# Projections and gates of three chunks in scaled fp16 parts, with the weights' parts kept in DRAM

## The chip, the cores and the metric

The kernel runs on one core of a Trainium2 chip. The metric is the time of one execution on the device in microseconds (us), the median of several runs. Engines are named as in the profile: PE (TensorE), PEld (its weight loads), DVE (VectorE), ACT (ScalarE), POOL (GpSimd) and SP (SyncE), which issues the DMAs.

## The reference, cut to what matters

One layer of a decoder trunk over 2048 tokens and 1024 channels, in float32. A normalised input h goes through one projection whose columns serve three token mixers and three merge gates; the three branches are merged by the gates, and a feed-forward part follows.

```python
h = rmsnorm(x, norm_mix_g[l])
proj = h @ w_in[l]
(lru_x, lru_gate, m_qk, m_v, m_o, m_i, m_f,
 s_q, s_k, s_v, g_a, g_b, g_c) = jnp.split(proj, split_points, axis=-1)
...
merged = (jax.nn.sigmoid(g_a) * ya + jax.nn.sigmoid(g_b) * yb
          + jax.nn.sigmoid(g_c) * yc)
x = x + merged @ w_o[l]

hf = rmsnorm(x, norm_ffn_g[l])
gate, up = jnp.split(hf @ w_ffn_in[l], 2, axis=-1)
x = x + (jax.nn.silu(gate) * up) @ w_ffn_out[l]
```

g_a, g_b and g_c are 1024 columns each, the other parts 2312 together.

## The kernel before, in words

The tokens are cut into four chunks of 512 (CH), the channels into eight groups of 128 (KT). Every product of the mixers works on two parts of each operand, a high and a low one, whose sum is the float32 value: `dense` (L194) issues three matmuls per group of channels, high by high, high by low, low by high, all in fp32r (the type that the program gives to 4-byte float operands of PE). A weight tile of 128 x 1024 holds one output group of 128 columns for all eight channel groups, so one output tile takes 24 matmuls of 512 columns.

`weights` (L183) makes the two parts of a weight tile: SP loads the raw tile (two buffers), ACT rounds it to the high part `wh` (L173), DVE subtracts to get the low part `wl` (L181); `wh` and `wl` have three buffers each. This happens anew for every chunk. `h_of_chunk` (L307) normalises the input of a chunk and splits it in the same way (`hh`, `hl`).

`S` (L313) makes the projections of a chunk: 14 tiles with `proj` (L336, weights wS, PSUM tile psd), and two token-major products with `tproj` (L342), in which a slice of h is the stationary operand and 264 columns (wMV) or 256 columns (wSV) of weights move; each of these has two weight tiles. So 18 weight tiles per chunk. In chunk 0 the input isn't normalised yet, and the results are scaled by the row R afterwards. The mLSTM, the LRU and the attention of the chunk before run beside it. `G` (L1042) makes the gates: for each of eight output groups one tile wY with the branches' outputs (py, six matmuls per branch), and for each of three branches one tile wG (pg, 24 matmuls), a sigmoid and the merge: 24 wG tiles per chunk. `G_out` (L1078) multiplies by wO (po) and adds the input. The feed-forward part (`F1`, `F2`) already works in fp16: `wforms` (L788) scales its weights by a power of two that is found from the sum of their squares (`squares`, `exponent`, `power`) and splits them with `split2` (L779) into two fp16 parts; `product` (L868) multiplies. Its input is prepared beside the gates of chunks 2 and 3 (`input_first`, L951: it loads fq with L944, DVE, POOL and ACT work on it).

The program is written as one sequence; a scheduler that knows each instruction's data and buffers then sets the order on every engine and on the DMA queue of SP. Pools of buffers set which tile waits for which reader. The instructions of each engine, and the DMAs that SP issues, stand in one line each.

Of the kernel before, what the change touches and what calls it, by code (L numbers as in the profile page):

```python
# [18 lines left out]
P = 128  # L19
# [15 lines left out]

class Trunk:
# [10 lines left out]
    def setup(self):  # L47
# [19 lines left out]
        self.dX1 = dr.tile([NCH, KT, P, CH], F32, name="dX1")  # L67
        self.dRow = dr.tile([NCH, 2, 4, CH], F32, name="dRow")
# [4 lines left out]
        self.rs2 = [cp.tile([P, NB], F32, name=f"rs2{c}") for c in range(NCH)]  # L73

# [104 lines left out]
    def split(self, hi, lo, src, eng, pool=False):  # L179
        self.hi(hi, src, eng)  # L180
        (self.nc.gpsimd if pool else self.nc.vector).tensor_tensor(lo, src, hi.bitcast(F32), op=ALU.subtract)  # L181

    def weights(self, src, ncol):  # L183
        wp = self.wp
        raw = wp.tile([P, WCOL], F32, tag="wraw", name="wraw", bufs=2)
        wh = wp.tile([P, WCOL], FR, tag="wh", name="wh", bufs=3)
        wl = wp.tile([P, WCOL], FR, tag="wl", name="wl", bufs=3)
        with self.first(self.HP & 1):
            self.nc.sync.dma_start(raw[:, :ncol], src)
            self.split(wh[:, :ncol], wl[:, :ncol], raw[:, :ncol], "P" if self.turn("wh", self.WH if self.phase == "S" else self.WG) else "A",  # L190
                       self.turn("wl", self.WL if self.phase == "S" else 0.0))
        return wh, wl

# [86 lines left out]
    def h_unscaled(self):  # L280
# [4 lines left out]
        for k in range(KT):  # L285
            if k % 4 == 2:
                self.w0.append(self.weights(self.I["wMV"][k // 4], 1056))
# [19 lines left out]
    def h_of_chunk(self, c):  # L307
# [3 lines left out]
        return self.make_h(p, lambda k: self.x_tile(c, k), self.g1, R, lambda k: [p.tile([P, CH], FR, tag="h" + e, name="h" + e, bufs=self.NH) for e in "hl"])  # L311

    def S(self, c, hs, at=None):  # L313
# [15 lines left out]
        def scaled(ps):  # L329
            if not at:  # L330
                return ps
            t = mp.tile([P, CH], F32, tag="cv", name="scl", bufs=1)
            V.tensor_tensor(t, ps, R, op=ALU.mult)  # L333
            return t

        def proj(i):  # L336
            w = self.weights(I["wS"][i], 1024)
# [4 lines left out]
        def tproj(name, n, per, after=None):  # L342
            pss = []
            ws = self.w0 if after else [self.weights(I[name][u], 4 * n) for u in range(2)]
# [25 lines left out]
        def mv(b, ps):  # L370
            r = rs[:, b : b + 1] if at else 1.0
# [7 lines left out]
        tproj("wMV", 264, mv, first_stat if at else None)  # L379
        st["vaug"], st["ifb"] = vaug, ifb  # L380

        def halo(tag, j, ps):
# [7 lines left out]
            else:  # L390
                A.activation(x[:, 3:], ps, AF.Copy)
# [12 lines left out]
        for j in range(4):  # L404
            x = halo("xm", j, proj(4 + j))
# [8 lines left out]
        for j in range(2):  # L414
            ps = scaled(proj(8 + j))
            o = mp.tile([P, CH], F32, tag=f"so{j}", name=f"so{j}", bufs=1)
            A.activation(o, ps, AF.Sigmoid)
            st["so"].append(o)
        def s_lru():
            st["xa"] = mp.tile([P, 2, CH], F32, tag="xa", name="xa", bufs=1)  # L420
            st["gl"] = mp.tile([P, 2, CH], F32, tag="gl", name="gl", bufs=1)
            for j in range(2):
                x = halo("xl", j, proj(10 + j))
                conv(st["xa"][:, j], x, self.cw_lru[:, j, :])
            for j in range(2):
                ps = scaled(proj(12 + j))
                t = mp.tile([P, CH], F32, tag="sg", name="gt", bufs=1)
                A.activation(t, ps, AF.Square)
# [3 lines left out]
                V.tensor_tensor(st["gl"][:, j], t, ps, op=ALU.mult)  # L432

        def s_sb():

            for i in range(4):
                ps = scaled(proj(i))
                th = mp.tile([P, CH], FR, tag="sth", name="sth", bufs=1)
                tl = mp.tile([P, CH], FR, tag="stl", name="stl", bufs=1)
                self.split(th, tl, ps, "A")  # L440
# [4 lines left out]
            def sv(b, ps):  # L445
                tv = mp.tile([P, 4, P], FR, tag="sth", name="sv", bufs=1)
                src = ps[:, :256]
                if at:
                    src = mp.tile([P, CH], F32, tag="cv", name="svs", bufs=1)[:, :256]
                    A.activation(src, ps[:, :256], AF.Copy, scale=rs[:, b : b + 1])  # L450
                src = src.rearrange("p (h d) -> p h d", h=4)
                self.split(tv[:, :, 0:64], tv[:, :, 64:128], src, "A")
                nc.sync.dma_start(self.dV[c * NB + b], tv.bitcast(F32))

            tproj("wSV", 256, sv)
# [265 lines left out]
    def F_constants(self):  # L721
# [13 lines left out]
        self.goff = row("goff", 197.0)  # L735
        self.gs2, self.offh2 = self.input_scale(self.g2, "2")
# [305 lines left out]
    def G(self, c, hs, steps=0):  # L1042
# [209 lines left out]
    def run(self):  # L1252
# [6 lines left out]
        with ExitStack() as s0:  # L1259
            with ExitStack() as s1:  # L1260
# [195 lines left out]
```

## Time and profile before

| | |
|---|---|
| median of 3 runs | 2951.1 us (2948.3 to 2951.5) |
| the profiled execution | 2951.2 us, its span 2949.5 us |
| PE busy | 2827.9 us, 96% of the span, 13409 matmuls |
| DVE busy | 1994.5 us, 68% |
| ACT busy | 1362.6 us, 46% |
| POOL busy | 782.2 us, 27% |
| read from and written to HBM | 310.9 MB and 87.6 MB |

The span goes from the first to the last instruction. The busy time of PE is modelled: matmuls follow each other in a pipeline and their records overlap, so that the pace of PE is read from the number of matmuls that start in a stretch, or from the starts themselves. In time the kernel has four parts: projections with the mixers to about 650 us (chunk 1 roughly from 150 to 310, chunk 2 to 485, chunk 3 to 650), the gates of chunks 0 and 1 beside the last attention to about 1115, the gates of chunks 1 to 3 with little beside them to about 1650, and the feed-forward part to the end.

### The profile page before, as it was taken

How to read it: one execution, taken by the hardware profiler on the slowest of the kernel's cores; microseconds unless marked ns; L12 is line 12 of the kernel's file. 1: busy time of each engine (PE TensorE's matmuls, PEld its weight loads, DVE VectorE, ACT ScalarE, POOL GpSimd, SP SyncE). 2: the span in 40 equal slices, each digit the busy share in tenths (PEclk: the TensorE clock that was granted, in tenths of full speed). 3: DMA queues.
4: the chain of work that ended last, by engine and by line, in shares of the span. 5: the costliest groups of instructions: out<-in, count | busy, mean ns of one | idle time of the engine just before them, and what ended most of it. 6: DMA issues, size and time to landing. Idle time of an engine off the chain costs nothing.

```text
span 2949.5 us, 37052 instructions
## 1 busy us (share of the span) xinstructions
PE 2827.9 (96%) x13409; PEld 1866.0 (63%) x13409; DVE 1994.5 (68%) x2933; ACT 1362.6 (46%) x2122; POOL 782.2 (27%) x916
## 2 busy tenths in 40 slices
PE   8999999998999999999999989999999999799996
PEld 7777878787887887878887534444444444344443
DVE  7678888988678775564444787556666665557557
ACT  4445554655455553333323466445554454335332
POOL 0122322332223220130001564223333333223221
PEclk9999999999999999999999999999999999999998
DMA  5445545345345325534433332122222226438324
GB/s 174 149 161 174 168 136 180 124 140 185 100 133 186 119 83 195 166 105 144 154 99 137 120 111 93 56 77 80 87 84 79 84 85 248 155 150 325 149 97 143
DMA packets 165271, 400.99 MB, mean 136 GB/s; under 512 B 19520, under 2 KB 40000, under 8 KB 156384
## 3 DMA queue, kind: packets, MB, share of 16 engines
q1 hardware_dynamic: 165088, 398.63, 39.5%
q8 instruction: 105, 1.72, 0.2%
q14 instruction: 78, 0.64, 0.1%
HBM read 310.93 MB, written 87.62 MB: 135 GB/s over the span
## 4 chain that ended last, share of the span: by engine, by line
PE 80%; DVE 8%; DMA 4%; issue 3%; ACT 2%; POOL 2%; SPq 0%; DVEq 0%; POOLq 0%; ACTq 0%
PE pfp L875 7%; PE pfp L876 7%; PE pfp L877 7%; PE pg L202 5%; PE pg L201 5%; PE pg L200 5%; PE pfq L875 3%; PE pfq L876 3%; PE pfq L877 3%; PE psd L200 3%; PE psd L202 3%; PE psd L201 3%; PE pt L707 2%; PE pfr L875 2%; PE pfr L876 2%
## 5 line engine op out<-in xcount | busy, mean ns | idle before, releaser
L181 DVE TENSOR_TENSOR wl<-wraw,wh 128x768 fp32r<-128x768 f32 (+2 forms) x232 | 287.5, 1240 | 245.7 <-ACT wh L173 237.7
L173 ACT ACTIVATE wh<-wraw 128x768 fp32r<-128x768 f32 (+2 forms) x232 | 238.9, 1030 | 433.8 <-PE pg L201 199.6
L875 PE MATMUL pfp<-f,wh 128*128 128x512 f16 x1056 | 403.3, 382 | 30.3 <-ACT wh L784 12.9
L876 PE MATMUL pfp<-f,wh 128*128 128x512 f16 x1056 | 403.2, 382 | 2.3 <-DVE f L782 2.3
L877 PE MATMUL pfp<-f,wl 128*128 128x512 f16 x1056 | 400.7, 381 | 0.0
L875 PEld LDWEIGHTS <-wh 128*128 128x128 f16 x1848 | 181.6, 98 | 248.7 <-ACT wh L784 19.1
L876 PEld LDWEIGHTS <-wh 128*128 128x128 f16 x1848 | 181.7, 98 | 235.1 <-issue 27.6
L877 PEld LDWEIGHTS <-wl 128*128 128x128 f16 x1848 | 181.4, 98 | 224.4 <-issue 9.0
L202 PE MATMUL pg<-hh,wl 128*128 128x512 f32 x768 | 307.1, 400 | 3.7 <-DVE wl L181 3.5
L200 PE MATMUL pg<-hh,wh 128*128 128x512 f32 x768 | 305.5, 398 | 3.1 <-ACT wh L173 3.1
L201 PE MATMUL pg<-hl,wh 128*128 128x512 f32 x768 | 305.7, 398 | 0.0
L802 POOL TENSOR_TENSOR sm<-raw 128x512 f32<-128x512 f32 (+1 forms) x50 | 67.5, 1350 | 592.7 <-DVE wl L785 271.7
L875 PE MATMUL pfq<-f,wh 128*128 128x512 f16 x528 | 201.5, 382 | 1.5 <-DVE xf L1188 1.0
L876 PE MATMUL pfq<-f,wh 128*128 128x512 f16 x528 | 201.4, 381 | 1.2 <-DVE f L782 1.2
L877 PE MATMUL pfq<-f,wl 128*128 128x512 f16 x528 | 200.4, 380 | 0.0
L200 PE MATMUL psd<-hh,wh 128*128 128x512 f32 x448 | 184.7, 412 | 3.2 <-DVE scl L333 2.7
L202 PE MATMUL psd<-hh,wl 128*128 128x512 f32 x448 | 180.1, 402 | 0.0
L201 PE MATMUL psd<-hl,wh 128*128 128x512 f32 x448 | 179.7, 401 | 0.0
L784 ACT ACTIVATE wh<-raw,scf 128x512 f16<-128x512 f32 (+1 forms) x166 | 127.1, 781 | 113.9 <-DVE scf L776 104.5
L202 PEld LDWEIGHTS pg<-hh,wl 128*128 128x128 f32 x768 | 145.5, 189 | 38.7 <-DVE wl L181 6.1
L200 PEld LDWEIGHTS pg<-hh,wh 128*128 128x128 f32 x768 | 146.3, 191 | 36.4 <-ACT wh L173 3.9
L201 PEld LDWEIGHTS pg<-hl,wh 128*128 128x128 f32 x768 | 145.6, 190 | 33.5
(318 smaller groups left out, 6232.9 us busy)
## 6 DMA issues: line engine op xcount, KB each, us to landing
wraw<-in_wG SPq DMA_DIRECT2D x96, 512.0 KB, 3.5
dA<-fs SPq DMA_DIRECT2D x154, 256.0 KB, 2.0
f<-dA SPq DMA_DIRECT2D x22, 1792.0 KB, 10.9
wraw<-in_wS SPq DMA_DIRECT2D x56, 512.0 KB, 3.8
raw<-in_wF SPq DMA_DIRECT2D x26, 1024.0 KB, 4.7
x<-in_xT SPq DMA_DIRECT2D x88, 256.0 KB, 3.8
wraw<-in_wO SPq DMA_DIRECT2D x32, 512.0 KB, 5.2
raw<-in_wP SPq DMA_DIRECT2D x16, 1024.0 KB, 6.7
```

Source lines behind the costliest of these rows:

```text
L173: nc.scalar.activation(dst, src, AF.Copy)
L181: (self.nc.gpsimd if pool else self.nc.vector).tensor_tensor(lo, src, hi.bitcast(F32), op=ALU.subtract)
L200: nc.tensor.matmul(ps, wh, hh, start=start and i == 0, stop=False)
L201: nc.tensor.matmul(ps, wh, hl, start=False, stop=False)
L202: nc.tensor.matmul(ps, wl, hh, start=False, stop=stop and i == n - 1)
L707: PE.transpose(pt[:, i * P : (i + 1) * P], As[i][:, js], self.idn)
L784: self.nc.scalar.activation(hi, x, AF.Copy, scale=s)
L802: G.tensor_tensor(sm[:, 0], a21, a22, op=ALU.add)
L875: mm(ps, wh[:, i, ks], f[:, j, 0], start=start and k == 0, stop=False, skip_group_check=True)
L876: mm(ps, wh[:, i, ks], f[:, j, 1], start=False, stop=False, skip_group_check=True)
L877: mm(ps, wl[:, i, ks], f[:, j, 0], start=False, stop=k == n - 1, skip_group_check=True)
```

## The change

Chunk 0 works as before, but ACT also squares each of its 42 raw tiles that chunks 1 to 3 use again (2 wMV, 2 wSV, 14 wS, 24 wG), into one column of `kacc` each. From these columns `weight_scales` finds a power of two per tile, in four calls: one small matmul with a tile of ones that sums over the partitions, and five to seven small DVE operations. `ksc` is the scale of a tile, `kinv` what its product is multiplied by.

In chunks 1 to 3 h is made in fp16 parts, with a scaled gain (`gs1`). Chunk 1 loads each raw tile, scales and splits it into two fp16 parts, both in one tile `w16`, and writes that tile to `dW` in DRAM. Chunks 2 and 3 load it from there, with one DMA of the same size as the raw tile; their buffers alternate between the two tags, six in all. What reads the products out of PSUM applies `kinv` as a scale: in ACT's activations and in DVE operations that take a factor. The products py and po, with wY and wO, stay as they were. The diff, cut to its core:

```diff
+        self.dW = dr.tile([NKEY, P, 2, WCOL], F16, name="dW")
...
-    def weights(self, src, ncol):
-        wp = self.wp
+    def weights(self, src, ncol, key=None, c=0):
+        nc, wp = self.nc, self.wp
+        if key is not None and c:
+            w = wp.tile([P, 2, WCOL], F16, tag="wl" if c > 1 and self.turn("w", 0.5) else "wh", name="w16", bufs=3)
+            wh, wl = w[:, 0, :ncol], w[:, 1, :ncol]
+            if c == 1:
+                raw = wp.tile([P, WCOL], F32, tag="wraw", name="wraw", bufs=2)
+                nc.sync.dma_start(raw[:, :ncol], src)
+                self.split2(wh, wl, raw[:, :ncol], self.ksc.bitcast(F32)[:, key : key + 1])
+                nc.sync.dma_start(self.dW[key, :, :, :ncol], w[:, :, :ncol])
+            else:
+                nc.sync.dma_start(w[:, :, :ncol], self.dW[key, :, :, :ncol])
+            return wh, wl
...
+        if key is not None:
+            self.squares(raw[:, :ncol], self.kacc[:, key : key + 1], raw[:, :ncol])
         return wh, wl
+
+    def weight_scales(self, k0, k1, pair=None):
+        nc, V = self.nc, self.nc.vector
+        n = k1 - k0
+        ps = self.psum("m", "pse")
+        nc.tensor.matmul(ps[:, :n], self.ones16, self.kacc[:, k0:k1], start=True, stop=True)
...
-        return self.make_h(p, lambda k: self.x_tile(c, k), self.g1, R, lambda k: [p.tile([P, CH], FR, tag="h" + e, name="h" + e, bufs=self.NH) for e in "hl"])
+        g, dt = (self.gs1, F16) if c else (self.g1, FR)
+        return self.make_h(p, lambda k: self.x_tile(c, k), g, R, lambda k: [p.tile([P, CH], dt, tag="h" + e, name="h" + e, bufs=self.NH) for e in "hl"])
...
-            w = self.weights(I["wS"][i], 1024)
+            w = self.weights(I["wS"][i], 1024, KS + i, c)
...
-                A.activation(x[:, 3:], ps, AF.Copy)
+                A.activation(x[:, 3:], ps, AF.Copy, scale=self.inverse(KS + i))
...
-                V.tensor_tensor(t, t, ps, op=ALU.mult)
+                V.scalar_tensor_tensor(t, ps, r, t, op0=ALU.mult, op1=ALU.mult)
...
-                w = self.weights(I["wG"][br * KT + j], 1024)
+                w = self.weights(I["wG"][br * KT + j], 1024, KG + br * KT + j, c)
...
-                    A.activation(sg, pg, AF.Sigmoid)
+                    A.activation(sg, pg, AF.Sigmoid, scale=self.inverse(KG + br * KT + j) if c else 1.0)
...
+                                    if c == 0:
+                                        self.weight_scales(KMV, KMV + 2, KMV)
+                                        self.weight_scales(KS + 4, KS + 14)
                                     st["sb"]()
+                                    if c == 0:
+                                        self.weight_scales(KSV, KS + 4, KSV)
...
+                    if c == 0:
+                        self.weight_scales(KG, NKEY)
                     self.G_out(c, mer, 3 if c == NCH - 1 else 0)
```

The scheduler orders the changed program anew. Two places on SP's queue show it. In the projections of chunk 1, toward the rows of the mLSTM (dRow), raw weight tiles (wraw) were loaded in a run, before:

```order
L189 DMA wraw<-in_wS 128x1024
L277 DMA x<-in_xT 128x512 x2
L189 DMA wraw<-in_wS 128x1024 x6
L558 DMA dRow<-sg 4x512
L559 DMA dRow<-yh 4x512
```

and now:

```order
L206 DMA dW<-w_2213 256x1x1024
L204 DMA wraw<-in_wS 128x1024
L206 DMA dW<-w_2253 256x1x1024
L204 DMA wraw<-in_wS 128x1024
L614 DMA dRow<-sg 4x512
L615 DMA dRow<-yh 4x512
```

Each load of a raw tile has got a write of fp16 parts (w with a number is the tile w16) just ahead of it.

At the start of the gates of chunk 2, where the input of the feed-forward part (fq) is loaded between the weights, before:

```order
L189 DMA wraw<-in_wY 128x768
L944 DMA fq<-dX_81 128x512
L189 DMA wraw<-in_wG 128x1024
L944 DMA fq<-dX_81 128x512 x2
L189 DMA wraw<-in_wG 128x1024
L944 DMA fq<-dX_81 128x512 x3
L189 DMA wraw<-in_wG 128x1024
```

and now:

```order
L208 DMA w_12534<-dW 128x2x1024
L1001 DMA fq<-dX_81 128x512 x2
L213 DMA wraw<-in_wY 128x768
L1001 DMA fq<-dX_81 128x512 x2
L208 DMA w_12586<-dW 128x2x1024
L1001 DMA fq<-dX_81 128x512 x2
L208 DMA w_12623<-dW 128x2x1024
```

The loads of wG have become reads of dW into the tiles that PE takes; they still share the queue with the loads of fq.

## Rows read from the trace of the kernel before

**Rows 1.** The page: busy us, share and instructions of each engine; the chain.
```profile
PE 2827.9 (96%) x13409; PEld 1866.0 (63%) x13409; DVE 1994.5 (68%) x2933; ACT 1362.6 (46%) x2122; POOL 782.2 (27%) x916
...
PE 80%; DVE 8%; DMA 4%; issue 3%; ACT 2%; POOL 2%; SPq 0%; DVEq 0%; POOLq 0%; ACTq 0%
```
**Rows 2.** By stage: us; PE, PEld, DVE, ACT, POOL busy (count); clock, DMA share, GB/s.
```profile
150.00:310.00 160.00, 151.35 (x806) 124.73 (x806) 124.24 (x201) 80.11 (x138) 45.09 (x75) 0.95 0.50 160
310.00:485.00 175.00, 167.47 (x901) 139.33 (x899) 146.22 (x226) 96.01 (x167) 51.93 (x91) 0.94 0.50 165
485.00:650.00 165.00, 159.49 (x858) 130.57 (x859) 144.02 (x216) 93.65 (x163) 47.81 (x90) 0.97 0.45 139
1450.00:1600.00 150.00, 150.00 (x646) 121.30 (x645) 59.41 (x72) 43.58 (x58) 0.00 (x0) 1.00 0.30 93
1800.00:2400.00 600.00, 599.88 (x2810) 272.07 (x2809) 371.86 (x558) 304.84 (x438) 191.34 (x136) 1.00 0.22 81
```
**Rows 3.** By stage, the scale sums (tile pse) on PE alone.
```profile
1800.00:2400.00 600.00, 5.68 (x34) 1.00 0.22 81
```
**Rows 4.** Groups of matmuls by line and form: busy us, mean ns, idle before.
```profile
L202 PE MATMUL pg<-hh,wl 128*128 128x512 f32 x768 | 307.1, 400 | 3.7 <-DVE wl L181 3.5
...
L200 PE MATMUL psd<-hh,wh 128*128 128x512 f32 x448 | 184.7, 412 | 3.2 <-DVE scl L333 2.7 <-DVE stl L181 0.5
...
L352 PE MATMUL psd<-wh,hh 128*128 128x264 f32 x128 | 40.6, 327 | 11.5 <-ACT wh L173 8.7 <-DVE ifb L373 2.4 <-ACT hh L173 0.4
```
**Rows 5.** PE in order of time, chunk 2's wMV: first and last of 18.
```profile
316.36 0.28 PE L353 MATMUL psd<-wl,hh 128*128 128x264 f32 x1
...
318.42 0.28 PE L352 MATMUL psd<-wh,hh 128*128 128x264 f32 x1
```
**Rows 6.** Groups: the two halves of a split, an accumulator's read, a scale sum.
```profile
L173 ACT ACTIVATE wh<-wraw 128x1024 fp32r<-128x1024 f32 x192 | 203.1, 1058 | 342.2 <-PE pg L201 175.1 <-PE psd L201 85.2 <-PE po L201 48.3
...
L181 DVE TENSOR_TENSOR wl<-wraw,wh 128x1024 fp32r<-128x1024 f32 x192 | 244.7, 1275 | 187.2 <-ACT wh L173 179.3 <-ACT yt L716 6.1 <-DMA dY<-ex 0.9
...
L756 ACT ACTIVATION_READ_ACCUMULATOR wl<-raw 128x1 bf16 x50 | 9.5, 190 | 0.0
...
L764 PE MATMUL pse<-wacc,ones 128*128 128x1 bf16 x50 | 8.3, 167 | 3.4 <-ACT wl L756 3.1 <-DVE rs L240 0.3
```
**Rows 7.** Waits of PE from 1230 to 1290 us (total, times, longest); two stretches by stage.
```profile
PE pg L200 <- ACT wh L173: 2.9, 1, 2.9
PE pg L202 <- DVE wl L181: 2.6, 1, 2.6
...
1255.00:1275.00 20.00, 14.51 (x49) 10.83 (x48) 18.45 (x18) 8.77 (x14) 13.44 (x8) 0.74 0.42 132
1280.00:1300.00 20.00, 19.85 (x86) 15.77 (x85) 12.16 (x14) 7.44 (x11) 4.61 (x3) 1.00 0.32 97
```
**Rows 8.** Waits of PE from 310 to 650 us, the first and the last of nine groups.
```profile
PE pt L707 <- DVE be L700: 3.0, 2, 1.8
...
PE psn L631 <- DVE ex L627: 0.3, 1, 0.3
```
**Rows 9.** Waits of SP's queue: at loads of raw weights, at a load of fq.
```profile
SPq L189 <- DVE wl L181: 547.3, 163, 9.6
...
SPq L944 <- POOL f L782: 6.9, 1, 6.9
```
**Rows 10.** DMAs: count, KB each, median us to landing; the tile wraw.
```profile
wraw<-in_wG SPq DMA_DIRECT2D x96, 512.0 KB, 3.5
...
x<-in_xT SPq DMA_DIRECT2D x88, 256.0 KB, 3.8
wraw<-in_wO SPq DMA_DIRECT2D x32, 512.0 KB, 5.2
...
L189 SPq DMA_DIRECT2D wraw<-in_wS x56: 327/333/688, 18.5 to 567.4; - x56
...
DMA to landing us min/median/max: 3.1/3.8/6.7
```

More of the change, by code (lines that the diff above doesn't have):

```diff
@@ L73, in setup @@
         self.rs2 = [cp.tile([P, NB], F32, name=f"rs2{c}") for c in range(NCH)]
+        self.kacc = cp.tile([P, NKEY], BF, name="kacc")
+        self.ksc = cp.tile([P, NKEY], I32, name="ksc")
+        self.kinv = cp.tile([P, NKEY], I32, name="kinv")
     def first_constants(self):
@@ L187, in weights, with inverse @@
         wl = wp.tile([P, WCOL], FR, tag="wl", name="wl", bufs=3)
[L188 to L191, printed above, removed]
+        nc.sync.dma_start(raw[:, :ncol], src)
+        self.split(wh[:, :ncol], wl[:, :ncol], raw[:, :ncol], "A")
+        if key is not None:
+            self.squares(raw[:, :ncol], self.kacc[:, key : key + 1], raw[:, :ncol])
         return wh, wl
+    def weight_scales(self, k0, k1, pair=None):
[3 more added lines that the diff above has]
+        nc.tensor.matmul(ps[:, :n], self.ones16, self.kacc[:, k0:k1], start=True, stop=True)
+        t = self.ksc[:, k0:k1]
+        V.tensor_scalar(t, ps[:, :n].bitcast(I32), 24, None, op0=ALU.logical_shift_right)
+        f = self.cp.tile([P, 24], F32, tag="ktf", name="ktf", bufs=1)[:, :n]
+        V.tensor_copy(f, t)
+        if pair is not None:
+            p = pair - k0
+            V.tensor_tensor(f[:, p : p + 1], f[:, p : p + 1], f[:, p + 1 : p + 2], op=ALU.max)
+            V.tensor_copy(f[:, p + 1 : p + 2], f[:, p : p + 1])
+        i = self.kinv[:, k0:k1]
+        V.tensor_scalar(i, f, 1.0, self.offh1[:, 1:2], op0=ALU.mult, op1=ALU.add)
+        V.tensor_scalar(i, i, 23, None, op0=ALU.logical_shift_left)
+        V.tensor_scalar(t, f, -1.0, 202.0, op0=ALU.mult, op1=ALU.add)
+        V.tensor_scalar(t, t, 23, None, op0=ALU.logical_shift_left)
+    def inverse(self, key):
+        return self.kinv.bitcast(F32)[:, key : key + 1]
     def dense(self, ps, w, terms, start=True, stop=True):
@@ L286, in h_unscaled @@
             if k % 4 == 2:
-                self.w0.append(self.weights(self.I["wMV"][k // 4], 1056))
+                self.w0.append(self.weights(self.I["wMV"][k // 4], 1056, KMV + k // 4))
             n = self.NBE
@@ L340, in proj, with tproj @@
             return ps
-        def tproj(name, n, per, after=None):
+        def tproj(name, n, key, per, after=None):
             pss = []
-            ws = self.w0 if after else [self.weights(I[name][u], 4 * n) for u in range(2)]
+            ws = self.w0 if after else [self.weights(I[name][u], 4 * n, key + u, c) for u in range(2)]
             for b in range(NB):
@@ L414, in S @@
         for j in range(2):
-            ps = scaled(proj(8 + j))
+            ps, r = scaled(8 + j)
             o = mp.tile([P, CH], F32, tag=f"so{j}", name=f"so{j}", bufs=1)
-            A.activation(o, ps, AF.Sigmoid)
+            A.activation(o, ps, AF.Sigmoid, scale=r)
             st["so"].append(o)
@@ L451, in sv @@
                 src = src.rearrange("p (h d) -> p h d", h=4)
-                self.split(tv[:, :, 0:64], tv[:, :, 64:128], src, "A")
+                th = tv[:, :, 0:64]
+                A.activation(th, src, AF.Copy, scale=r)
+                V.scalar_tensor_tensor(tv[:, :, 64:128], src, r, th.bitcast(F32), op0=ALU.mult, op1=ALU.subtract)
                 nc.sync.dma_start(self.dV[c * NB + b], tv.bitcast(F32))
-            tproj("wSV", 256, sv)
+            tproj("wSV", 256, KSV, sv)
         st["lru"], st["sb"] = s_lru, s_sb
```

38 lines of the change are left out of this document (23 added, 15 removed).

## Prediction

> **What bounds the kernel now.** I read the page's busy shares and its chain first, then busy time by stage, then single instructions. TensorE is busy 96% of the span, and the chain that ended last is 80% TensorE; VectorE follows with 68% busy and 8% of the chain [rows 1]. A busy TensorE is modelled, so I looked for its real pace in the table by stage [rows 2]. From 1450 to 1600 us, gates of chunk 3 alone, 646 matmuls start in 150 us, one each 0.232 us, at granted clock 1.00 and with DVE and ACT at 40% and 29%: nothing but the matmuls themselves sets that time. From 1800 to 2400 us, the feed-forward part, 2810 start in 600 us; 34 of them are the tiny scale sums [rows 3], so 2776 matmuls of 512 columns take 0.216 us each. Same shape, same clock (1.00, the level of 2.4 GHz): the one stage has fp32r operands, the other fp16. That difference of 0.016 us is what the change is after. In the stages of chunks 1 to 3 before 650 us [rows 2] the clock is 0.94 to 0.97 and DVE is busy 78, 84 and 87% of the time: there TensorE also waits, and a shorter matmul need not show in full.
>
> **Wide matmuls, removed cost.** The gates are three lines of 768 matmuls, the projections three of 448 [rows 4], in four chunks. Three of the four chunks change: 3 x 768 x 3/4 = 1728 and 3 x 448 x 3/4 = 1008, together 2736. At 0.0161 us each (0.2322 less 0.2161) that is **44.1 us**, 27.8 us of it in the gates and 16.2 in the projections. The products py (wY) and po (wO) stay in fp32r.
>
> **Narrow matmuls.** The two token-major products have h as the stationary operand and 264 or 256 columns of weights moving. Steady, 17 intervals between the two rows shown take 2.06 us, so 0.1212 us for 264 columns [rows 5], within 0.002 us of 264/512 of the wide one. No fp16 matmul of that width is in the trace. If fp16 costs by the column as it does at 512, it takes 0.111 us and saves 0.0098 each; if a fixed part stands in the way (its weight load can't hide) it saves nothing; if it saves as much as a wide one, 0.016. There are six groups of 128 matmuls, three lines at each of two widths ([rows 4] show one), and three quarters of them change: 576. I take the proportional value, **5.6 us**, since the fp32r pair already is proportional; bounds 0 and 9.3.
>
> **Splitting that goes.** Chunks 2 and 3 no longer split: per chunk 18 projection tiles and 24 gate tiles, 84 in all, each 1.058 us on ACT and 1.275 us on DVE [rows 6]: 89 and 107 us of work. Nearly all of it lay beside the matmuls. Two places where it didn't:
> - At the start of chunk 2's gates TensorE waits 2.9 us for an ACT half and 2.6 us for a DVE half of a wG tile, behind the normalisation of the feed-forward input on the same engines. In the 20 us around it 49 matmuls start against 86 in a like stretch just after, and the clock is 0.74 [rows 7]: 37 matmuls, 8.6 us. In the changed kernel that tile is read ready from DRAM. I take **8 us**; bounds 0 (the read is late instead) and 8.6.
> - In the projections of chunks 2 and 3 the waits of TensorE between 310 and 650 us are for other work, DVE's above all: nine groups from 3.0 down to 0.3 us [rows 8], 13 us together. The granted clock is 0.94 and 0.97 there [rows 2], so part of the time at 1.2 GHz in place of 2.4: (1 - 0.94) x 175 + (1 - 0.97) x 165 = 15 us more. DVE loses 36 x 1.275 = 46 us of its 290 us, 16%. If the waits shrink in proportion, 16% of 28 us: **4 us**; bounds 0 and 28.
>
> **What is added.** In chunk 0 each of 42 tiles is squared on ACT. The pass over 1024 columns is 1.058 us and reading the accumulator 0.19 us [rows 6], 52 us together; ACT has 46% busy over the span [rows 1] and gives back 89 us later, so it lies beside the matmuls. If that cover were gone it would cost up to 52 us. Four sums of exponents are put into TensorE's queue, each 0.167 us, and can wait for the last square: 50 such sums waited 3.4 us together [rows 6]. I take **+2 us**; bounds 1 and 14 (four waits as long as all of those 50 together).
> In chunk 1 the split stays and 42 writes are added, 22 MB. On SP each stands just ahead of the load of a raw tile. Both wait for the same split, because that load needs the raw buffer that the split frees: already before, SP waited 163 times, 547 us in all, at that load for the DVE half [rows 9]. The write adds no wait in the queue, only its issue, 0.33 us for a raw load [rows 10], and the transfer; I take 0, bounded above by 42 x 0.33 = 14 us.
> In chunks 2 and 3 84 reads of the same size come instead of the raw loads. A raw tile of 512 KB lands in 3.5 us (wG) or 5.2 us (wO), any raw tile in 3.1 to 6.7; x, in rows of 2 KB as the new tiles have them, takes 3.8 us for half as much [rows 10]. A gate branch is 24 x 0.216 + 6 x 0.232 = 6.6 us, and by the order of the code the scarcest buffer comes back a branch and the six py before it is needed, 8.0 us. So a read is hidden when it lands in less than 8; I take 0.
> The evictions with a scale, the fp16 halves of h and the two fused products with PSUM are the same counts on the same engines; an fp16 write by DVE is in the profile already, and I cost them at nothing, beside TensorE.
>
> **Sum.** -44.1 - 5.6 - 8 - 4 + 2 = -59.7. The profiled execution took 2951.2 us (span 2949.5 and 1.7 around it), as good as the median of 2951.1, so **2891 us**. After 1720 us nothing changes but what the scheduler shifts, and I leave that stage as it is.
>
> **Rivals.**
> 1. *Projections don't gain.* With DVE at 78 to 87% in chunks 1 to 3, shorter matmuls there may only wait longer for the scans and the halves of attention, whose amount is unchanged. Then the gates' 27.8 and the 8 us are left: 2951 - 36 = 2915. For it: the DVE column of [rows 2]. Against: TensorE's own waits there are short [rows 8], and DVE loses 16% in chunks 2 and 3.
> 2. *The waits go, too.* DVE's queue is a single line; if its relief takes most of the 28 us of waits and half clock, 2891 - 20 = 2871. Against: 84 tiles fewer don't touch chunk 1, and the longest waits are for attention's own chain.
> 3. *The width doesn't matter.* The 0.016 us might belong to the stage, not the type. Then only the 8 and 4 us less 2 are left: 2941. Against it are the two steady stretches [rows 2] at the same clock, and DVE and ACT are busier in the faster one. The Trainium skill states this rival as a rule (TensorE: Matmul & The Clock Gate, Weight-path perf modes): the array takes one element per cell and cycle whatever its width. By that rule the wide matmuls would save nothing; the two stretches speak against it by 7%.
> 4. *The other side: SP's queue makes the reads late.* A read of dW has no raw tile loaded ahead of it and stands in one line with DMAs that wait for other engines: at the start of chunk 2's gates behind the loads fq, which waited up to 6.9 us for POOL, elsewhere behind writes that wait for DVE, where SP stood up to 9.6 us [rows 9]. Behind the longest, a read lands 9.6 + 3.8 - 8.0 = 5.4 us late, with TensorE idle meanwhile. From twelve such on, the 60 us are gone; with twenty of the 84 late the kernel takes 2891 + 108 = 2999. Against: 9.6 us is the longest of 163, and the scheduler puts each DMA where it expects its source ready.
>
> **Numbers.** The forecast (2891, its own bounds about 2877 to 2905) gets 0.66, rival 1 0.16, rival 2 0.10, rival 3 0.03, rival 4 0.05. The range runs from below rival 2 to above rival 1: 2862 to 2922; outside it lie rivals 3 and 4 and the tails. A measurement of this kernel can tell about 0.2%, 6 us, from no change. Faster by more than that are all but rival 4 and a sliver of unforeseen cost: 0.93; the same 0.02; slower 0.05.
>
> **What would show it.** In the changed profile: TensorE's starts in the gates of chunks 1 to 3 at about 0.216 us in place of 0.232, those of chunk 0 unchanged; narrow ones near 0.111; no wait for a weight half at the start of chunk 2's gates; SP's waits for PE at the reads of dW without TensorE waiting for them; DVE some 100 us and ACT some 40 us less busy in sum. Wrong it would be by starts of 0.232 in the fp16 gates, by waits of TensorE for dW (rival 4), by a longer stage from 150 to 310 us, chunk 1, with its split and its writes (rival 1), or by new waits in chunk 0 for the squares.

## The result and the profile after

The changed kernel takes **2920.3 us** (median of 4 runs, 2914.5 to 2921.4), the kernel before 2951.3 in the same job: a ratio of 0.9899, 95% interval 0.9887 to 0.9911. That is 31 us where 60 were forecast. The profiled execution has a span of 2919.0 us.

The page, busy time of each engine, answers to [rows 1]:

```profile
PE 2789.9 (96%) x13414; PEld 1597.4 (55%) x13414; DVE 1900.0 (65%) x2882; ACT 1340.0 (46%) x2123; POOL 755.2 (26%) x917
```

DVE has 94.5 us less to do and ACT 22.6, against some 100 and 40 forecast. TensorE is as full as before: its work got shorter, but not its share.

Groups of matmuls, the fp16 ones of the gates and of the projections, against [rows 4] (busy us, mean ns, idle before):

```profile
L248 PE MATMUL pg<-hh,w 128*128 128x512 f16 x576 | 219.5, 381 | 5.5 <-ACT w L841 3.5 <-ACT sgg L1121 2.1
...
L248 PE MATMUL psd<-hh,w 128*128 128x512 f16 x336 | 130.2, 387 | 1.2 <-DVE ifb L424 0.7 <-ACT x L443 0.5
```

Narrow ones in order of time, first and last of 18 in chunk 2, against [rows 5]:

```profile
322.82 0.29 PE L403 MATMUL psd<-w,hh 128*128 128x264 f16 x1
...
324.74 0.28 PE L405 MATMUL psd<-w,hl 128*128 128x264 f16 x1
```

17 intervals in 1.92 us: 0.113 us each for 264 columns, where fp32r took 0.121. From one start to the next the wide fp16 ones take 0.216 us in gates and projections alike. So the price of each wide matmul came out as forecast; the narrow ones take 0.113 us where 0.111 was forecast.

By stage (us; PE, PEld, DVE, ACT, POOL busy; clock, DMA share, GB/s), against [rows 2]:

```profile
150.00:310.00 160.00, 145.80 (x812) 90.76 (x810) 118.32 (x196) 81.22 (x129) 34.66 (x60) 0.93 0.71 238
310.00:485.00 175.00, 166.49 (x984) 106.11 (x984) 133.42 (x225) 85.14 (x162) 50.42 (x106) 0.97 0.55 175
485.00:650.00 165.00, 157.47 (x838) 96.80 (x837) 122.25 (x193) 74.73 (x138) 36.90 (x88) 0.93 0.39 123
...
1800.00:2400.00 600.00, 600.00 (x2811) 272.34 (x2810) 363.76 (x551) 298.55 (x427) 188.43 (x134) 1.00 0.21 79
```

The feed-forward part kept its pace. In the projections the granted clock is lower than before in two of the three stretches, and TensorE's time without a matmul is longer in all three (14.2, 8.5 and 7.5 us against 8.6, 7.5 and 5.5): shorter matmuls, longer gaps. (The stretches are cut at fixed times, and chunks 1 to 3 lie some 10 us later in them than before.) Read from single instructions, before and after:

| milestone | before | after | moved |
|---|---|---|---|
| last projection of chunk 0 | 150.9 | 165.1 | +14.2 |
| last projection of chunk 3 | 642.4 | 653.6 | +11.2 |
| gates of chunk 0, last matmul | 891.2 | 887.8 | -3.4 |
| gates of chunk 1, first to last | 208.2 | 210.0 | +1.8 |
| gates of chunk 2, first to last | 177.0 | 159.1 | -17.9 |
| gates of chunk 3, first to last | 166.8 | 156.0 | -10.8 |
| last product po of chunk 3 | 1656.7 | 1626.7 | -30.0 |

The gates of chunks 2 and 3 gained what was forecast (9.3 each, and 8 for the stall). The rows add up only with a stretch whose arithmetic is unchanged: from the last projection of chunk 3 to the last matmul of chunk 0's gates 14.6 us less pass than before, so what the projections lost was made good there; how is not shown. At the start of chunk 2's, where [rows 7] had waits of 2.9 and 2.6 us for weight halves, the waits of PE from 1195 to 1300 us are one line:

```profile
PE pg L248 <- ACT sgg L1121: 2.1, 2, 1.9
```

Chunk 0, whose arithmetic is unchanged, lost 14 us. The waits of TensorE that the trace lists from 40 to 180 us sum to 14.0 us, before to 10.1. Some of them, and the two longest of ACT from 0 to 150 us (total, times, longest):

```profile
PE psd L248 <- DVE ksc L237: 3.7, 1, 3.7
...
PE psl L536 <- ACT lr L534: 2.1, 1, 2.1
PE psd L403 <- ACT svs L504: 2.0, 2, 1.3
```

```profile
ACT wh L183 <- PE psd L249: 15.4, 4, 6.2
ACT wraw L813 <- DVE wl L192: 11.5, 8, 2.8
```

ACT's wait for PE is not new (21.1 us before); its wait at L813, the square, is. The square is written over the raw weight, so it waits until DVE has used the raw weight for the low half, which shows for eight of the 18 squares in this stage. ACT in order of time, from one high half to the next (start, duration, in brackets the idle time before it and its releaser):

```profile
44.70 1.04 ACT L183 ACTIVATE wh<-wraw 128x1024 fp32r<-128x1024 f32 x1
47.44 1.06 ACT L813 ACTIVATE wraw<-wraw 128x1024 f32<-128x1024 f32 x1 [1.70 <-DVE wl L192]
48.41 0.18 ACT L813 ACTIVATION_READ_ACCUMULATOR wraw<-wraw 128x1 bf16 x1
48.50 1.04 ACT L183 ACTIVATE wh<-wraw 128x1024 fp32r<-128x1024 f32 x1
```

Between one high half and the next 3.8 us pass, 1.7 of them idle, in a queue in which the mixers' sigmoids and copies out of PSUM stand as well.

By themselves these waits are not the loss. By 90 us TensorE has started 336 of the projections' matmuls in either kernel, and the high half that ACT starts at 88.5 us before starts at 91.1 us now. The loss comes right behind. The projections' matmuls (tile psd) on TensorE in two stretches, then all engines from 95 to 122 us, before and after (clock, DMA share and GB/s at the end):

```profile
0.00:90.00 90.00, 73.40 (x336) 0.98 0.50 169
90.00:120.00 30.00, 12.31 (x43) 0.89 0.26 84
...
95.00:122.00 27.00, 27.00 (x142) 21.82 (x141) 20.59 (x39) 12.72 (x17) 3.19 (x2) 0.87 0.29 100
```

```profile
0.00:90.00 90.00, 73.84 (x336) 0.98 0.48 164
90.00:120.00 30.00, 0.31 (x1) 0.59 0.15 53
...
95.00:122.00 27.00, 26.22 (x98) 19.84 (x99) 17.32 (x36) 11.17 (x16) 1.02 (x1) 0.51 0.13 46
```

From 89.4 to 119.7 us TensorE has no matmul of the projections, only those of the mixers and of the normalisation, most of them of 128 columns or fewer. Before, this pause of the projections took 15 us, and projections stood between the rest of that work. And now TensorE does the work almost wholly at 1.2 GHz (granted clock 0.51, before 0.87). From these clocks, as an estimate, (0.87 - 0.51) x 27 = 10 us of the 14 are lost here. Just before the clock falls, TensorE waits 2.1 us for lr (the line psl above; 0.7 before), and a square with its wait for DVE stands ahead of lr in ACT's queue. That the squares bring this stretch about is likely, since another order with squares has it too (the changed kernel with a tiny store, below: clock 0.52). Why the clock stays down for so long is not shown.

The reads of written weights did no harm: TensorE waits for one of the 84, and that 0.3 us, though SP's queue stands long before them, for TensorE to free the buffers (SP's waits from 1170 to 1620 us, against [rows 9]; then the DMA group, against [rows 10]):

```profile
SPq L208 <- PE pg L250: 121.0, 25, 6.0
SPq L213 <- DVE wl L192: 101.2, 31, 10.0
```

```profile
w<-dW SPq DMA_DIRECT2D x80, 512.0 KB, 4.5
```

### The profile page after: what moved, and what is told of

Read it like the earlier page. It is cut to its first block, busy times and chain, and to the rows that moved or that the text cites. A ratio compares the mean times of both kernels' runs of the same rounds, so it can differ in the third digit from the quotient of the medians.

```text
span 2919.0 us, 36923 instructions
## 1 busy us (share of the span) xinstructions
PE 2789.9 (96%) x13414; PEld 1597.4 (55%) x13414; DVE 1900.0 (65%) x2882; ACT 1340.0 (46%) x2123; POOL 755.2 (26%) x917
## 5 line engine op out<-in xcount | busy, mean ns | idle before, releaser
L248 PE MATMUL pg<-hh,w 128*128 128x512 f16 x576 | 219.5, 381 | 5.5 <-ACT w L841 3.5
L249 PE MATMUL pg<-hl,w 128*128 128x512 f16 x576 | 218.8, 380 | 0.0
L250 PE MATMUL pg<-hh,w 128*128 128x512 f16 x576 | 218.2, 380 | 0.2 <-DVE w L842 0.2
L192 DVE TENSOR_TENSOR wl<-wraw,wh 128x1024 fp32r<-128x1024 f32 (+2 forms) x106 | 126.5, 1195 | 53.7 <-ACT wh L183 32.0
L813 ACT ACTIVATE wl<-raw 128x2048 uint8<-128x2048 f32 (+1 forms) x50 | 91.9, 1838 | 145.3 <-issue 77.0
L1121 ACT ACTIVATE sgg<-pg,kinv 128x512 f32<-128x512 f32 x72 | 49.5, 688 | 236.8 <-PE pg L250 236.8
L842 DVE SCALAR_TENSOR_TENSOR wl<-raw,scf,wh 128x512 f16<-128x512 f32 (+1 forms) x166 | 138.2, 842 | 29.8 <-ACT wh L841 29.5
L248 PEld LDWEIGHTS <-w 128*128 128x128 f16 x912 | 89.8, 99 | 118.7 <-issue 22.2
L250 PEld LDWEIGHTS <-w 128*128 128x128 f16 x912 | 90.0, 99 | 108.0 <-issue 8.7
L183 ACT ACTIVATE wh<-wraw 128x1024 fp32r<-128x1024 f32 (+2 forms) x106 | 105.1, 993 | 91.1 <-PE po L249 32.8
L249 PEld LDWEIGHTS <-w 128*128 128x128 f16 x912 | 90.0, 99 | 102.3 <-issue 11.9
```

Source lines behind the costliest of these rows:

```text
L183: nc.scalar.activation(dst, src, AF.Copy)
L248: nc.tensor.matmul(ps, wh, hh, start=start and i == 0, stop=False)
L249: nc.tensor.matmul(ps, wh, hl, start=False, stop=False)
L250: nc.tensor.matmul(ps, wl, hh, start=False, stop=stop and i == n - 1)
L813: self.nc.scalar.activation(junk, src, AF.Square, accum_out=acc)
L842: self.nc.vector.scalar_tensor_tensor(lo, x, s, hi, op0=ALU.mult, op1=ALU.subtract)
```

## The experiments

All ratios are to the kernel before, run in the same job (its medians 2948.7 to 2951.4); a ratio of 0.0010 is 3 us. The scatter of the order comes first, since every small difference has to stand against it.

**One tiny store at the start**, in the kernel before and in the changed one:

```diff
+        nc.vector.memset(cp.tile([P, 4], F32, name="nudge"), 0.0)
```

> The kernel before with one small store to an unused tile on DVE at its start. It changes what the scheduler knows by some tens of ns, and so a part of the order. Theory: order alone moves the time by up to 5 us: 2944 to 2955 us. More than that, and the differences of a few us between the other runs tell nothing.

> The changed kernel with the same small store at its start. Theory: 2914 to 2926 us. Below 2910 us, and the cost that I put down to the squares would be an accident of one order.

Measured: 2952.3 us, 1.0008 (0.9997 to 1.0019), and 2922.4 us, 0.9905 (0.9892 to 0.9919). Two or three us from the order alone; the cost in chunk 0 is there again (its last projection is 15.6 us later than before).

### What the added work costs

**A constant scale**: no squares, no sums.

```diff
-            self.squares(raw[:, :ncol], self.kacc[:, key : key + 1], raw[:, :ncol])
...
-        nc.tensor.matmul(ps[:, :n], self.ones16, self.kacc[:, k0:k1], start=True, stop=True)
...
-        V.tensor_scalar(t, ps[:, :n].bitcast(I32), 24, None, op0=ALU.logical_shift_right)
...
+        nc.gpsimd.memset(f, 67.0)
...
```

> The changed kernel with a constant scale for the fp16 parts: it leaves out finding the scales, that is the 42 squares of chunk 0 on ACT, the sums of them on PE and the reading of their exponents. The rest of the scale's small operations on DVE stays. If the work that finds the scales has eaten the projections' gain (theory A: the projections' end came 14.2 us later than before in chunk 0, and their gain of 16 us was lost there), the last matmul of chunk 0's projections comes back by some 11 to 14 us and the whole time is about 2908 us. If shorter matmuls in the projections only wait longer for the mixers' DVE and ACT work (theory B: the stage is not bound by PE's pace), chunk 0 gets its 11 to 14 us back, but the later chunks give most of it back in waits, and the time is 2917 to 2921 us.

Measured: 2904.6 us, 0.9848 (0.9835 to 0.9861), somewhat below what theory A said. The added work costs 0.0051, **15 us**.

**The added work alone**, in fp32r arithmetic:

```diff
     def weights(self, src, ncol, key=None, c=0):
+        if c:
+            key = None
...
     def inverse(self, key):
+        return 1.0
...
-        g, dt = (self.gs1, F16) if c else (self.g1, FR)
+        g, dt = self.g1, FR
```

> The arithmetic of the kernel before in all chunks (weights and inputs of projections and gates in fp32r parts, no weights written to DRAM) with the work that finds the scales added: 42 squares on ACT in chunk 0, their sums and the small operations; nothing uses the scales. Theory A: the added work costs 11 to 14 us at the end of chunk 0's projections and nothing later gives it back, so 2962 to 2965 us. Theory B (the stage waits for DVE and ACT in any case, and what is late in chunk 0 is made up in the slack of chunks 1 and 2): 2951 to 2955 us.

Measured: 2970.2 us, 1.0072 (1.0060 to 1.0085): 21 us, more than A said (2962 to 2965 us), and nothing later makes it good. B falls as an account of chunk 0's loss.

**Squares or sums.** One run keeps the squares with the constant scale, the other keeps sums and chains, of a constant, without the squares (the diff is the second's):

```diff
+        nc.gpsimd.memset(self.kacc, 1.0)
...
-            self.squares(raw[:, :ncol], self.kacc[:, key : key + 1], raw[:, :ncol])
+            pass
```

> As the run with a constant scale (2904.6 us), but with the 42 squares on ACT kept, unused; the sums on PE and the reading of exponents are left out, as there. It divides the 14 us by which the last matmul of chunk 0's projections moved between the changed kernel and the one with the constant scale. If the squares on ACT are what costs (theory A1): 2915 to 2920 us. If it is the sums and the chains of small DVE operations, behind which the copies out of PSUM queue (theory A2: the changed kernel has a wait of 3.9 us at 59.7 us on such a chain): 2904 to 2908 us.

> As the changed kernel, with the sums on PE and the chains of small operations that make the scales, but without the 42 squares on ACT: the sums are taken of a constant, so the scale found is a constant. Theory A1 (the squares cost the 14 us): 2904 to 2908 us. Theory A2 (the sums and chains do): 2915 to 2920 us.

Measured: with the squares 2927.4 us, 0.9925 (0.9912 to 0.9939); with the sums 2904.2 us, 0.9851 (0.9835 to 0.9868). Of the two, A1 holds: it is the squares, though the first time lies above A1's range of 2915 to 2920. The first has less to do than the changed kernel, but for four small fills on POOL, and took 0.0026 longer, 7 us: likely the order, as the intervals hardly part and its five executions run from 2916.8 to 2929.2 us.

**The square's place and size.** Squares in a tile of their own (in bfloat16; the diff is this run's); over 128 columns in place; over 128 columns in a tile of their own:

```diff
-            self.squares(raw[:, :ncol], self.kacc[:, key : key + 1], raw[:, :ncol])
+            n = min(ncol, 1024)
+            sq = wp.tile([P, 1024], BF, tag="sq", name="sq", bufs=1)
+            self.squares(raw[:, :n], self.kacc[:, key : key + 1], sq[:, :n])
```

> The squares cost some 16 us: 2920.3 with them, 2904.6 and 2904.2 without. Their own time on ACT among chunk 0's projections is 19 us and 3.4 us for reading the sums, and ACT stands 11.5 us in front of them until DVE has made the same weight's low half, because each square is written over the raw weight that DVE still reads. In this kernel the changed one's squares go to a tile of their own (over 1024 columns, so 16 of a 1056-column weight's last block are left out of its sum), and wait for nothing but the raw weight. If the wait in front of the squares is what costs (theory A3): 2905 to 2911 us. If their 22 us of work on ACT is (theory A4): 2917 to 2921 us.

> The changed kernel with squares over the first 128 columns of a weight, still written over the raw weight. Their work in chunk 0's projections falls from 22 to about 9 us, the wait for DVE's low half stays. A3 (the wait costs): 2916 to 2921 us. A4 (the work costs): 2906 to 2911 us.

> Squares over the first 128 columns of a weight, written to a tile of their own: both the wait and most of the work are gone. A3 and A4 both say 2904 to 2909 us. If it is 2915 us or more, neither is the reason, and the squares cost by their place in the order alone.

Measured: own tile 2907.6 us, 0.9865 (0.9847 to 0.9883); short in place 2910.4 us, 0.9868 (0.9853 to 0.9882); both 2906.4 us, 0.9860 (0.9842 to 0.9877). Either alone gives back about 10 us, both together hardly more. So neither A3 nor A4 is right alone. What moves with the time is the pause of the projections from about 90 us on. It takes 30 us in the changed kernel, 28 in the run with the added work alone, 19 with the squares in their own tile, 17 with short ones in place, 14 with both, and 17 with the constant scale (15 before). The granted clock from 95 to 122 us is 0.51, 0.60, 0.75, 0.81, 0.94 and 0.83 in these runs (0.87 before). It isn't all, for the run with unused squares has a pause of 18 us and the time above. The loss can be read at the end of chunk 0's wide projections and the start of chunk 1's narrow ones (instructions of the tile psd, with their first and last start), in the changed kernel, with the constant scale, and with the full squares in their own tile:

```profile
L403 PE MATMUL psd<-w,hh x192: 269/276/437, 169.4 to 653.4; 128*128 128x264 f16 x96, 128*128 128x256 f16 x96
...
L248 PE MATMUL psd<-hh,wh x112: 389/393/774, 23.3 to 150.2; 128*128 128x512 f32 x112
```

```profile
L399 PE MATMUL psd<-w,hh x192: 269/276/427, 160.7 to 638.4; 128*128 128x264 f16 x96, 128*128 128x256 f16 x96
...
L244 PE MATMUL psd<-hh,wh x112: 388/393/774, 22.5 to 140.2; 128*128 128x512 f32 x112
```

```profile
L405 PE MATMUL psd<-w,hh x192: 269/276/443, 155.9 to 642.2; 128*128 128x264 f16 x96, 128*128 128x256 f16 x96
...
L250 PE MATMUL psd<-hh,wh x112: 388/393/797, 23.5 to 142.5; 128*128 128x512 f32 x112
```

The wide ones end at 150.2, 140.2 and 142.5 us. With a tile of its own the square stands ahead of the high half and waits for the raw weight's load alone (ACT from 0 to 150 us):

```profile
ACT sq L815 <- DMA wraw<-in_wS: 13.2, 8, 3.6
```

That the wait for DVE is gone is shown, but ACT doesn't stand less: 13.2 us for loads at the squares and 3.1 at the high halves, against 11.5 and 4.0 in the changed kernel. And with short squares in place the wait for DVE grows, to 17.8 us in 11 waits, while the time falls. So the sum of ACT's waits doesn't set the time; how the square's place and size change the pause is not shown.

**Three or six buffers in chunk 1**, alone, with short squares, one sum for all projections' scales and six buffers, and with the short squares in their own tile:

```diff
-tag="wl" if c > 1 and self.turn("w", 0.5) else "wh"
+tag="wl" if self.turn("w", 0.5) else "wh"
```

> The changed kernel with chunk 1's fp16 weights in six buffers instead of three, as chunks 2 and 3 have them. The gates of chunk 1 gained under 2 us of the 9.3 forecast, with waits for the split's halves at 1136 to 1142 us. If three buffers, each held until its write to DRAM has landed, cause this (theory C1): the gates of chunk 1 gain 5 to 8 us more, about 2913 to 2916 us. If it is the order of the work on ACT and DVE there (theory C2): 2919 to 2921 us.

> Six buffers in chunk 1, squares over the first 128 of a weight's 1024 columns only (a scale from fewer elements, still found on the chip), and one sum for all projections' scales instead of three. By A1 an eighth of the columns leaves about a third of the squares' time on ACT (a fixed part stays), so 8 to 10 of the 14 us come back: 2910 to 2912 us, and with C1's 5 to 8 us 2903 to 2906 us. By A2 one chain instead of three gives back some 9 us, about the same, so the run with squares alone tells these two apart, not this one. Under 2918 us, the time with fp16 in the gates alone, it is the better version.

> As the run with short squares in a tile of their own (2906.4 us), with six buffers for chunk 1's fp16 weights. Theory C1 (three buffers cost in chunk 1's gates): 2899 to 2903 us. Theory C2 (they don't): 2903 to 2911 us, the scatter of the order alone.

Measured: 2921.6 us, 0.9903 (0.9889 to 0.9917); 2917.9 us, 0.9895 (0.9882 to 0.9909); 2905.9 us, 0.9856 (0.9840 to 0.9872). C1 falls: the time gains nothing by the buffers. In the first of the three the gates of chunk 1 do take 10 us less than in the changed kernel (200.0 us from first to last), but they begin 10 us later; with three buffers and short squares in their own tile they take 200.4. Over the runs with fp16 gates the stage takes from 200 to 211 us; that it depends on how much of the mixers' work is left for it is a guess. The second run is a miss that stays open: it should have been near the run with short squares in place (0.9868), and has the single sum besides.

### What the parts are worth

**Gates alone and projections alone** (the other half in fp32r, without its squares and sums):

```diff
+        if key is not None and key < KG:
+            key = None
...
```

> fp16 parts in the gates alone; the projections of all chunks as before in fp32r parts, without their 18 squares and their three sums; the gates' 24 squares stay in chunk 0's gates. From the milestones of the two traces the gates gave 28 us between the start of chunk 0's gates and the end of chunk 3's (17 in chunk 2, 9.5 in chunk 3, under 2 in chunk 1). Theory A: the same gates here, and no delay in chunk 0's projections: 2920 to 2926 us. Theory B says the same of this kernel, since it speaks of the projections alone. A time of 2935 us or more would say that the gates' gain needs the projections' change.

> fp16 parts in the projections of chunks 1 to 3 alone, with their 18 squares and three sums in chunk 0 and their weights through DRAM; the gates as before in fp32r parts. My forecast's terms for this half were 16.2 us for 1008 wide matmuls, 5.6 for 576 narrow ones and 4 for waits, with 2 for the added work: 2927 us. Theories A and B both say that nearly nothing of it is left, by the milestones 0 to 5 us: 2946 to 2951 us. Where the work goes tells them apart: by A the last matmul of chunk 0's projections is 11 to 14 us late and those of chunks 1 to 3 gain as much again; by B chunk 0's is hardly late, and the chunks 1 to 3 gain nothing.

Measured: gates alone 2918.0 us, 0.9899 (0.9886 to 0.9911), projections alone 2944.8 us, 0.9991 (0.9976 to 1.0006). Both are 1 or 2 us under what the theories said. The gates' half is worth 30 us, all that the whole change gives; the projections' half pays for its own squares and no more. In the former's profile the gates of chunks 1 to 3 take 7.8, 17.9 and 10.8 us less than before, 36.5 together, and the stretch from chunk 3's last projection to chunk 0's last gate is as long as before (249.2 and 248.8 us): the 14.6 us made good there in the changed kernel belong to the projections' half. In the latter's the last projection of chunk 0 is 16.4 us later than before and that of chunk 3 only 3.3: A's picture, with the gain made afterwards and lost beforehand. (That execution took 2938.9 us, 6 less than the median of a run that scatters from 2935 to 2961.)

**A third of the projections' matmuls left out** in chunks 1 to 3, on top of the constant scale; the token-major products lose theirs in the same way:

```diff
-            nc.tensor.matmul(ps, wl, hh, start=False, stop=stop and i == n - 1)
+            if not two:
+                nc.tensor.matmul(ps, wl, hh, start=False, stop=stop and i == n - 1)
...
```

> The run with the constant scale (2904.6 us), with the product of the weights' low half and the inputs' high half left out of the projections of chunks 1 to 3: 336 matmuls of 512 columns and 192 of 264 or 256 are gone, 336 x 0.216 + 192 x 0.111 = 94 us of PE's work. If PE's pace sets the projections, nearly all of it comes off: about 2815 us. If the mixers' chains on DVE and ACT set a floor (theory B), a good part is given back in waits, in the projections and in the gates that follow: 2835 to 2875 us. The fp16 parts took 13.4 us off (2918.0 with the gates alone, 2904.6 with both and a constant scale) where 22 us of matmul time went, a share of six tenths; the same share of 94 us is 57 us, so 2847 us.

Measured: 2875.4 us, 0.9752 (0.9738 to 0.9765): 0.0096 or 28 us of the 94. That is the far end of what B said, and the share of six tenths was too much: seven tenths of what was taken out come back, as waits and as time at the lower clock. The stage of chunk 1 and the longest waits of TensorE from 150 to 640 us in that run:

```profile
150.00:310.00 160.00, 128.03 (x640) 78.02 (x639) 121.27 (x204) 84.85 (x147) 48.34 (x81) 0.82 0.70 231
```

```profile
PE pt L761 <- DVE be L754: 11.1, 6, 5.4
PE psd L400 <- DVE stl L491: 6.7, 4, 4.8
PE pav L768 <- DVE al L192: 6.5, 6, 2.1
PE psd L400 <- DVE ifb L422: 6.3, 3, 3.3
```

TensorE is busy 128 of 160 us, and the mean granted clock is 0.82, where the run with the constant scale has 0.94, so a part of the rest runs at 1.2 GHz. The four longest waits are for DVE.

**No trip through DRAM**: with short squares in their own tile (0.9860), every chunk splits all weights again; then only the projections' (the diff is this run's), then only the gates':

```diff
-            if c == 1:
+            if c == 1 or key < KG:
...
-                nc.sync.dma_start(self.dW[key, :, :, :ncol], w[:, :, :ncol])
+                if not (key < KG):
+                    nc.sync.dma_start(self.dW[key, :, :, :ncol], w[:, :, :ncol])
```

> As the run with short squares in a tile of their own (2906.4 us), but no weights are written to DRAM: chunks 2 and 3 split every weight again, as chunk 1 does. If reading the parts is worth what I forecast (theory D1: 8 us for the stall of the kernel before at the start of chunk 2's gates, 4 us for other waits for the split's halves in the projections, and more where DVE and ACT bound the stage, since 28 splits of projection weights at 2.3 us on ACT and DVE come back there): 2916 to 2930 us. If the splits were hidden and the stall was an accident of the order (theory D2): 2904 to 2910 us.

> As the run with short squares in a tile of their own (2906.4 us), with the projections' weights of chunks 2 and 3 split again and only the gates' read from DRAM. With fp32r projections and fp16 gates the time was 2918.0 us. Theory E1 (the projections gain nothing by their matmuls' width, only by the ACT and DVE work that reading takes away): 2916 to 2924 us. Theory E2 (they gain by width, 10 us or more): 2905 to 2911 us.

> The reverse: the projections' weights of chunks 2 and 3 are read, the gates' split again in every chunk. E1, with 15 of the 20.8 us in the projections: 2910 to 2914 us. E2: most of the 20.8 us sits in the gates, 2920 to 2926 us.

Measured: all 2927.2 us, 0.9921 (0.9909 to 0.9933); projections 2924.3 us, 0.9910 (0.9895 to 0.9924); gates 2913.5 us, 0.9867 (0.9850 to 0.9885). By their times D1 and E1 hold, the second run 0.3 us above E1's range; but D1's 8 us for the stall are not there, since reading the gates' weights is worth 0.0007, 2 us. Reading is worth 0.0061, 18 us, and nearly all of it, 0.0050 or 15 us, comes with the projections' weights. Chunk 2's projections by stage, read and split again:

```profile
310.00:470.00 160.00, 152.80 (x858) 95.76 (x858) 113.00 (x197) 71.74 (x132) 34.38 (x82) 0.94 0.51 162
```

```profile
310.00:470.00 160.00, 151.30 (x831) 94.06 (x830) 131.48 (x212) 88.42 (x144) 42.48 (x74) 0.93 0.51 166
```

The same 160 us hold 858 matmuls in one and 831 in the other, with DVE busy 113 and 131 us, ACT 72 and 88. The count of matmuls in a fixed stretch is a weak sign: 15 us longer, to 485 us, it is 912 and 933. The ends tell more. Chunk 2's last projection starts at 469.4 and 474.0 us, chunk 3's at 641.8 and 650.6, so some 9 of the 15 us are there. Most of the rest shows in the gates of chunk 1, 200.4 and 210.6 us from first to last, whose weights are split in both; why is not shown.

And with the projections in fp16 but split in every chunk (0.9910) the kernel is no faster than with fp32r projections (0.9899): there the shorter matmuls are worth nothing that can be measured. The comparison isn't of width alone. The fp16 kernel has 18 short squares and their sums besides, and its splits cost more, 1.145 us on ACT and 1.339 on DVE for 1024 columns, against 1.058 and 1.275 [rows 6]. And no run reads fp32r parts from DRAM, so what the width is worth where weights are read is not shown.

## Why the prediction was wrong

The time lies inside the range, near its upper end; the forecast case was wrong by half. Rival 1, with a chance of 0.16 and 2915 us, was nearest. It knew one of the two reasons, and came as near as it did by luck: the squares cost about what reading in the projections gave, 15 us each, and it had neither.

- **Wide matmuls in the gates, 27.8, and the stall, 8.** The sizes were right: 35.8 forecast, 30 measured for the gates' half, and 36.5 in the gates of its profile. In the changed kernel's profile chunks 2 and 3 gave 17.9 and 10.8 us, chunk 1 nothing. The mechanism holds for the width, not for the stall: it went, but mostly not because the weights are read. Split again, chunk 2's gates still take only 161.9 us, against 177.0 before and 159.3 when read.
- **Projections, 16.2 and 5.6 for the matmuls' width.** This step failed. Each matmul is as short as forecast, but the sum took matmuls saved times their price as time saved, in stages where DVE was busy 78 to 87% [rows 2]. I had written that a shorter matmul need not show in full there, and counted it in full. Measured: nothing with the splits kept, and 28 us of 94 in the run with a third left out. At 22 us this is the largest miss.
- **Waits in the projections, 4.** Mis-sized: about 15, of which 9 show by the end of the projections. The proportional rule, 16% less DVE work so 16% less waiting, was too tame: 36 splits fewer are 46 us of DVE's and 38 of ACT's time, and the rule left ACT out.
- **Squares, +2.** This step failed too: 15 to 21 measured, outside the bounds of 1 and 14, where the value taken was that of the sums, which cost about 1 us (each with six or eight small DVE operations, not five to seven). The sign named for it, new waits in chunk 0 for the squares, came. The 52 us of ACT were called hidden because ACT is busy 46%. The average was not at fault: from 0 to 150 us, where 18 of the 42 squares fall, ACT was busy 68 us before, 46% too. What the step left out is the order. In ACT's queue the squares stand ahead of high halves and of the mixers' steps that TensorE waits for, and eight of the 18 wait for DVE themselves. In the profile the loss shows in one stretch of 30 us in which TensorE has no projections to do and most of the time only 1.2 GHz: by the estimate above, 10 of chunk 0's 14 us. That the squares cost the time is shown by the runs without them; how they bring that stretch about stays open.
- **Writes and reads, 0.** Right for the reads: 0.3 us of waiting for them in all, and rival 4 did not come. No run leaves out the writes alone, so their 0 is not tested.
- **Rival 3**, the pace that doesn't depend on width, is out by the starts: 0.216 us in the fp16 gates, 0.233 in chunk 0's fp32r ones, at clock 1.00. The Trainium skill (TensorE: Matmul & The Clock Gate, Weight-path perf modes) has the array take one element per cell and cycle at any width; this trace disagrees by 7%, and the trace decides.

With measured sizes the sum closes: gates -30, width in the projections 0 (+3 as measured), reading there -15, the added work +15, together -27 to -30, where 0.9899 is -30. With 2 to 7 us from the order alone it could have missed by as much.

The better version comes out of this: squares over 128 columns, written to a tile of their own, 2906.4 us, 0.9860; with six buffers besides 2905.9 us, 0.9856, which is no different.

## What to carry to other kernels

Price a shorter matmul stage by stage: where TensorE's gaps end on another engine, work taken from that engine can pay more than a shorter matmul, and here reading ready weights in place of splitting them paid what the projections' shorter matmuls did not. Added work isn't hidden just because its engine is idle half of the time: ask what stands behind it in that engine's queue, and look at the granted clock where TensorE comes to wait. An output that nobody reads is better given a place of its own: written over an operand that another engine is reading, it waits for that engine (11.5 us here). Before a difference of a few us is explained, move the order a little and see what that alone does.

## What the runs showed beyond the question

A 512-column matmul costs 0.232 us in fp32r and 0.216 in fp16, one of 264 columns 0.121 and 0.113, all at granted clock 1.00 or close to it: a saving by the column, with no fixed part that shows. A stage in which TensorE was given less to do lost part of it through the clock (0.82 in place of 0.94). The granted clock can also stay down while TensorE is busy: from 95 to 122 us of the changed kernel it is 0.51, with TensorE shown busy for 26.2 of the 27 us. And a kernel with work taken out was slower than the one with it (2927.4 against 2920.3 us, the run with unused squares), which I put down to the order; that wasn't tried.
